# Token blocks of a Strassen-like gate and up product, built in four interleaved steps, and two VectorE operands read from PSUM

## The chip, the cores and the metric

The kernel runs on one core of one Trainium2 chip. The metric is the device time of one execution in microseconds (us); the number given for a kernel is the median of its runs. Engines are named as in the profile: PE is TensorE (matmuls), PEld its weight loads, DVE is VectorE, ACT is ScalarE, POOL is GpSimd, SP the engine whose queue issues the DMAs.

## What is computed

One layer of a streaming encoder on x of 512 tokens by 2048 channels, float32. The part that matters here is its end:

```python
y = jnp.concatenate([y_sb, y_cv, y_sg], axis=-1)          # each normalised per head
x = x + jnp.einsum('bse,ed->bsd', y, w_out[l])            # 2048 x 2048
h = rms_norm(x, ffn_norm[l])
gate = causal_depthwise_conv(jnp.einsum('bsd,df->bsf', h, w_gate[l]), ffn_conv_w[l], ffn_conv_b[l])
up = jnp.einsum('bsd,df->bsf', h, w_up[l])                # d = 2048, f = 5632
x = x + jnp.einsum('bsf,fd->bsd', jax.nn.silu(gate) * up, w_down[l])
return rms_norm(x, final_norm)
```

## The kernel before

Every float32 operand of a matmul is used as two parts, `hi` (the value rounded to TensorE's fp32r format by a cast on ScalarE) and `lo` (value minus `hi`, a subtraction on VectorE), and every product is three matmuls: hi·hi, lo·hi, hi·lo. `split` makes the two parts; `mm3` issues the three matmuls. For sums of weights `make_split` casts twice on ScalarE, once to SBUF (`b_hi`, the operand) and once to a PSUM bank (`b_hp`), and VectorE subtracts the PSUM copy; for raw weights there is one cast and VectorE reads `b_hi` from SBUF.

The W_out stage runs over four blocks `nb` of 512 output columns, each over 16 row blocks of the contraction (`rows_by_weight`, results in four PSUM banks called `po`, of ring `zz` or `mm` in turn). At the end of a block VectorE adds the banks to x, giving `x1[nb][tt]`, ScalarE squares each tile with a sum (`add2`, for the token statistics; the squares go to a tile `junk` that nobody reads), and the tile is stored to DRAM for the last stage.

Gate and up multiply in the Winograd form of Strassen's scheme: seven products of half-size blocks in place of eight. The weight side's sums S1 to S4 are made on GpSimd (`make_sum`). The token side needs, for each of 8 row blocks j, the blocks R11, T1 (`build_a`) and R21, R22, T2, T3, T4 (`build_b`). `build_b(j)` transposes x1 on TensorE (`turned`, tile `ps_tr`), scales it out of PSUM on ScalarE (`f_b`), splits that into `rb`, forms T3 = R22 - R12 on GpSimd and T2 = R22 - T1 on VectorE (tile `t_b`), splits that into `rc`, forms T4 = R21 - T2 and splits it into `rd`. `build_a` of all j and `build_b` of j = 0 to 3 run beside the W_out products (table `WHEN`); `build_b` of j = 4 to 7 needs the last x1 block and is called whole, two blocks ahead of the first product, one after product n = 0 and one after n = 1 (`more_rows`).

The products run over 44 groups g of 256 columns, gate and up in turn, and in a group over 14 half products (i = 0 to 6 of `SEQ`, q = 0 or 1, each 12 matmuls). `order` lists them; its first 28 mix the first two groups so that half products that need late blocks come later. In step n the program issues the weight sum six ahead, the split four ahead, the product, `more_rows(n)` and the steps of the output generators (`gate_out`, `up_out`). The sums X, Y, Z1, Z2 of a group share two PSUM banks; after i = 2 ScalarE copies X to c11 and VectorE adds Y; after i = 3 VectorE makes c22 from Z1 and Z2; after i = 4 ScalarE copies X to u (`ff_u`) and VectorE adds u to c22; c12 and c21 follow from u and Z1, Z2 (all c tiles are called `ff_g` in the trace). i = 4 adds into X again, so it may start only when c11 is out.

ScalarE's instructions stay in program order (`keep_in_program_order`); the order on the other engines and on the DMA queue is set by the framework's scheduler from ready times that it reckons itself. The line that records every engine operation is 105, so groups are told apart by tile names. `token_row` (at n = 6) turns the token statistics (`fin2`, on GpSimd) into `row2`, with eight small matmuls `ps_row`; the gate outputs are multiplied by it.

Of the kernel before, what the change touches and what calls it, by code (L numbers as in the profile page):

```python
# [9 lines left out]
F32 = mybir.dt.float32  # L10
F32R = mybir.dt.float32r
AF = mybir.ActivationFunctionType
ALU = mybir.AluOpType
# [100 lines left out]
def trunk_kernel(  # L114
# [128 lines left out]
    def split(hi, lo, src, hi_eng=None, lo_eng=None):  # L243
        if hi_eng is None:
            act_.copy(hi, src)
        else:
            hi_eng.tensor_copy(hi, src)
        return (lo_eng or vec).tensor_tensor(out=lo, in0=src, in1=hi.bitcast(F32), op=ALU.subtract)
# [106 lines left out]
    def token_stats(name, junk_tile):  # L355

        ssq = const.tile([P, NT, 4], F32, name=f"ssq_{name}")
        rs = const.tile([P, NT], F32, name=f"rstd_{name}")

        def add(tt, b, src):  # L360
            act_.activation(junk_tile(), src, AF.Square, accum_out=ssq[:, tt, b : b + 1])
            return ssq[:, tt, b : b + 1]

        def finish_(tt):
            acc = ssq[:, tt, :]
            pool.tensor_tensor(out=acc[:, 0:2], in0=acc[:, 0:2], in1=acc[:, 2:4], op=ALU.add)
            pool.tensor_tensor(out=acc[:, 0:1], in0=acc[:, 0:1], in1=acc[:, 1:2], op=ALU.add)
            rstd_cols(rs[:, tt : tt + 1], acc[:, 0:1], D)

        return rs, add, finish_  # L370
# [475 lines left out]
        exp_ln_table()  # L846
        iss.spawn(gate_u(half, u), w)

    rstd2, add2, fin2 = token_stats("x1", lambda: tmp("junk"))
    x1 = [[None] * NT for _ in range(4)]  # L850
    x1_dram = [[dram.tile([P, S], F32, name=f"x1_{nb}_{tt}") for tt in range(NT)] for nb in range(4)]

# [13 lines left out]
    tmp_pool = raw_pool = x1_pool = act2 = None  # L866

    def tmp(name):
        return tmp_pool.tile([P, S], F32, tag="tmp", bufs=12, name=name)


    groups = [(w, 256 * fp) for fp in range(NF // 2) for w in (w_gate, w_up)]
# [29 lines left out]
            return act_tile(name)  # L902
        return x1_pool.tile([P, S], F32R, tag="x1", bufs=8, name=name)

    def turned(kt, tag_fn, name):
        ps = tag_fn("ps_tr")
        for tt in range(NT):
            transpose(ps[:, tt * P : (tt + 1) * P], x1[kt // 4][tt][:, (kt % 4) * P : (kt % 4 + 1) * P], ident)
        f = tmp(name)
        act_.activation(f, ps, AF.Copy, scale=gcol(32 + kt))  # L910
        return f

    def halves_of(t):
        return t[:, 0:HT], t[:, HT:S]

    def build_a(j, tag_fn):

        fa[j] = f = turned(j, tag_fn, "f_a")
        hi, lo = r_tile("ra_hi", True), r_tile("ra_lo", True)
        f0, f1 = halves_of(f)  # L920
        for at, name in enumerate(("R11", "T1")):
            if at:
                vec.tensor_tensor(out=f0, in0=f1, in1=f0, op=ALU.subtract)
            h, l = halves_of(hi)[at], halves_of(lo)[at]
            split(h, l, f0)
            R[name, j] = (h, l)

    def build_b(j, tag_fn):

        f, t = turned(j + 8, tag_fn, "f_b"), tmp("t_b")  # L930
        t1, r12 = halves_of(fa.pop(j))
        r21, r22 = halves_of(f)
        t2, t3 = halves_of(t)
        hi, lo = r_tile("rb_hi"), r_tile("rb_lo")
        split(hi, lo, f)
        R["R21", j], R["R22", j] = zip(halves_of(hi), halves_of(lo))
        pool.tensor_tensor(out=t3, in0=r22, in1=r12, op=ALU.subtract)
        vec.tensor_tensor(out=t2, in0=r22, in1=t1, op=ALU.subtract)
        hi, lo = r_tile("rc_hi"), r_tile("rc_lo")
        split(hi, lo, t)  # L940
        R["T2", j], R["T3", j] = zip(halves_of(hi), halves_of(lo))
        vec.tensor_tensor(out=r21, in0=r21, in1=t2, op=ALU.subtract)
        h, l = halves_of(r_tile("rd"))
        split(h, l, r21)
        R["T4", j] = (h, l)

    WHEN = {1: {3: 0, 6: 1, 9: 2, 12: 3}, 2: {3: 4, 6: 5, 9: 6, 12: 7}, 3: {2: 0, 5: 1, 8: 2, 11: 3}}
    for nb in range(4):
        tag_fn, other = (mm, zz) if nb % 2 == 0 else (zz, mm)
        banks = [tag_fn("po") for _ in range(NT)]  # L950
        for n, kt in enumerate(OUT_ORDER):
            if nb == 0 and n + 4 < KT:
                out_operand(OUT_ORDER[n + 4])
            rows_by_weight(banks, yT[kt], n == 0, n == KT - 1)
            if nb == 0 and n == KT - 5:
                open_up_stage()
            if n in WHEN.get(nb, ()):
                (build_b if nb == 3 else build_a)(WHEN[nb][n], other)
            if n == KT - 5:
                for tt in range(NT):  # L960
                    x1[nb][tt] = x1_pool.tile([P, S], F32, tag="x1", bufs=8, name="x1")
                    nc.sync.dma_start(out=x1[nb][tt], in_=x[tt * P : (tt + 1) * P, nb * S : (nb + 1) * S])
        for tt in range(NT):
            vec.tensor_tensor(out=x1[nb][tt], in0=x1[nb][tt], in1=banks[tt], op=ALU.add)
            if nb < 3:
                add2(tt, nb, x1[nb][tt])
            nc.sync.dma_start(out=x1_dram[nb][tt], in_=x1[nb][tt])
        if nb == 2:
            blk_load(0)
    mix_stage.close()  # L970
    sp = up_stage.enter_context(tc.tile_pool(name="split", bufs=1, reuse_waits="tile"))

# [18 lines left out]
    def make_sum(n):  # L991
        g, i, q = UNITS[n]
        name = SEQ[i][0]
        if name in SUMS:
            a, b, op = SUMS[name]
            if g == 1 and (name == "S1" or (name, q) == ("S3", 0)):
                t = tmp("b_sum").rearrange("p (k c) -> p k c", k=4)
            else:
                t = sp.tile([P, 4, P], F32, tag="sum", bufs=5, name="b_sum")
            pool.tensor_tensor(out=t, in0=operand(g, a, q), in1=operand(g, b, q), op=op)  # L1000
            sums[g, name, q] = t

    def make_split(n):
        g, i, q = UNITS[n]
        if i == 0 and q == 0 and g > 0:
            blk_load(g + 1)
        hi = sp.tile([P, 4, P], F32R, tag="bhi", bufs=5, name="b_hi")
        lo = sp.tile([P, 4, P], F32R, tag="blo", bufs=4, name="b_lo")
        src = operand(g, SEQ[i][0], q)
        if SEQ[i][0] in SUMS:  # L1010


            hp = zz("b_hp").rearrange("p (k c) -> p k c", k=4)
            act_.copy(hi, src)
            act_.copy(hp.bitcast(F32R), src)
            vec.tensor_tensor(out=lo, in0=src, in1=hp, op=ALU.subtract)
        else:
            split(hi, lo, src)
        parts[n] = (hi, lo)
# [35 lines left out]
    def product(n):  # L1055
        g, i, q = UNITS[n]
        if g not in banks_of:
            b1, b2 = mm("pt"), mm("pt")
            banks_of[g] = (*halves_of(b1), *halves_of(b2))
        X, Y, Z1, Z2 = banks_of[g]  # L1060
        acc = (X, Z1, Y, Z2, X, Z1, Z2)[i]
        hi, lo = parts.pop(n)
        for kk in range(4):
            rh, rl = R[SEQ[i][1], 4 * q + kk]
            mm3(acc, hi[:, kk, :], lo[:, kk, :], rh, rl, i < 2 and q == 0 and kk == 0, q == 1 and kk == 3)
        if q == 0:
            return
        if i < 2:
            return
        if g not in outs_of:  # L1070
            outs_of[g] = (tmp("ff_g0"), tmp("ff_g1"))
        (c11, c12), (c21, c22) = (halves_of(c) for c in outs_of[g])
        f0 = 2 * (g // 2)
        out_fn = gate_out if g % 2 == 0 else up_out
        if i == 2:
            act_.copy(c11, X)
            vec.tensor_tensor(out=c11, in0=c11, in1=Y, op=ALU.add)
        elif i == 3:
            vec.tensor_copy(c22, Z1)
            vec.tensor_tensor(out=c22, in0=c22, in1=Z2, op=ALU.add)  # L1080
        elif i == 4:
            u_of[g] = tmp("ff_u")[:, 0:HT]
            act_.copy(u_of[g], X)
            vec.tensor_tensor(out=c22, in0=c22, in1=u_of[g], op=ALU.add)
        elif i == 5:
            vec.tensor_tensor(out=c12, in0=u_of[g], in1=Z1, op=ALU.add)
            out_steps.append(out_fn(f0, outs_of[g][0]))
        elif i == 6:
            vec.tensor_tensor(out=c21, in0=u_of[g], in1=Z2, op=ALU.add)
            out_steps.append(out_fn(f0 + 1, outs_of[g][1]))  # L1090
# [17 lines left out]
    blk_load(1)  # L1108
    for n in range(AHEAD):
        make_split(order[n])  # L1110
    build_b(4, zz)
    build_b(5, zz)
    row2 = None

    def more_rows(n):
        nonlocal row2
        if n == 0:
            build_b(6, zz)
        elif n == 1:
            for tt in range(NT):  # L1120
                add2(tt, 3, x1[3][tt])
            build_b(7, zz)
        elif n == 6:
            for tt in range(NT):
                fin2(tt)
            row2 = token_row(rstd2, "x1")
# [163 lines left out]
```

## Time and profile before

| | |
|---|---|
| runs | 2257.87, 2253.45, 2257.39 us; median 2257.39 |
| profiled execution | 2258.5 us; its span on the core 2256.8 us |
| mean granted clock of TensorE | 0.989 of full speed |
| busy | PE 2144.6 us (95%), PEld 1936.0 (86%), DVE 1507.1 (67%), ACT 1213.2 (54%), POOL 777.3 (34%) |
| chain that ended last | PE 83%, DVE 8%, ACT 4%, issue 2%, POOL 1%, DMA 1% |
| DMA | 245.29 MB, mean 109 GB/s; q1 32.8% of 16 engines |
| PE in 40 slices, tenths | 8999999999999879999999999999999799999998 |

A busy share is an average over stages; a slice is 56.4 us. The W_out stage ends near 771 us, gate and up run to about 1730, the down projection to the end. In a list of waits a line reads: engine, tile and line that waited, whom it waited for, us in total, times, the longest. In a timeline the bracket behind an instruction is the idle time of its engine before it and what ended that.

### The profile page before, as it was taken

To read this page: it belongs to the slowest core of one execution; us is meant where nothing else is said; L and a number is where in the kernel's file an instruction comes from. 1 tells how busy PE (TensorE), PEld (TensorE's weight loads), DVE (VectorE), ACT (ScalarE), POOL (GpSimd) and SP (SyncE) were. 2 spreads that over 40 slices of the span, in tenths; PEclk is the share of its full clock that TensorE was granted. 3 is DMA by queue.
4 is the path that set the end of the run, shared out by engine and by line. 5 is a ranking of instruction groups with operands and counts; after the bars stand their busy time and mean duration, and the time that the engine had idled before them with its cause. 6 is when DMAs were issued, how large, how long until landed. Compare 5 with 4: busy or idle time off the path is not lost.

```text
span 2256.8 us, 36249 instructions
## 1 busy us (share of the span) xinstructions
PE 2144.6 (95%) x13529; PEld 1936.0 (86%) x13529; DVE 1507.1 (67%) x2264; ACT 1213.2 (54%) x2260; POOL 777.3 (34%) x699
## 2 busy tenths in 40 slices
PE   8999999999999879999999999999999799999998
PEld 6888888798788779999999999999999688888886
DVE  4789897977734667777777777777777444343335
ACT  5335567676634466666676666666666332232223
POOL 1021232321300356566566566656755000000002
PEclk9999999999999989999999999999999899999999
DMA  5232222222264123333323323333331844332232
GB/s 177 92 94 77 65 75 66 66 61 66 85 220 154 66 72 99 121 105 111 118 94 127 113 94 127 103 109 116 100 122 48 289 150 132 111 122 98 99 108 98
DMA packets 193890, 245.29 MB, mean 109 GB/s; under 512 B 8901, under 2 KB 140849, under 8 KB 193713
## 3 DMA queue, kind: packets, MB, share of 16 engines
q1 hardware_dynamic: 193153, 242.70, 32.8%
q8 instruction: 106, 1.74, 0.3%
q14 instruction: 71, 0.58, 0.1%
q10 hardware_dynamic: 560, 0.27, 0.0%
HBM read 223.01 MB, written 19.92 MB: 108 GB/s over the span
## 4 chain that ended last, share of the span: by engine, by line
PE 83%; DVE 8%; ACT 4%; issue 2%; POOL 1%; DMA 1%; SPq 0%; DVEq 0%; POOLq 0%; ACTq 0%
PE pt L172 48%; PE pd L172 19%; PE po L172 8%; PE pn L172 3%; PE pl L172 2%; DVE cv_acc L105 1%; DVE b_lo L105 1%; DVE w_lo L105 1%; DVE ff_g L105 1%; ACT e L105 1%; PE av L172 1%; PE z_C L172 1%; PE z_A L172 0%; DVE wt_lo L105 0%; PE z_B L172 0%
## 5 line engine op out<-in xcount | busy, mean ns | idle before, releaser
L105 DVE TENSOR_TENSOR w_lo<-w_raw,w_hi 128x512 fp32r<-128x512 f32 x400 | 284.7, 719 | 345.8 <-ACT w_hi L105 342.3
L105 ACT CAST w_hi<-w_raw 128x512 fp32r<-128x512 f32 x400 | 245.3, 621 | 455.5 <-PE pd L172 308.6
L105 DVE TENSOR_TENSOR b_lo<-b_sum,b_hp 128x512 fp32r<-128x512 f32 x352 | 239.6, 685 | 152.1 <-PE pt L172 122.8
L105 DVE TENSOR_TENSOR b_lo<-b_raw,b_hi 128x512 fp32r<-128x512 f32 x264 | 279.6, 1083 | 26.2 <-PE pt L172 17.3
L105 ACT CAST b_hi<-b_sum 128x512 fp32r<-128x512 f32 x352 | 218.1, 620 | 135.6 <-PE pt L172 60.8
L172 PE MATMUL pd<-w_hi,t_hi 128*128 128x512 f32 x640 | 250.3, 391 | 14.2 <-ACT w_hi L105 14.2
L172 PE MATMUL pd<-w_lo,t_hi 128*128 128x512 f32 x640 | 250.1, 391 | 0.0
L172 PE MATMUL pd<-w_hi,t_lo 128*128 128x512 f32 x640 | 249.9, 391 | 0.0
L105 POOL TENSOR_TENSOR b_sum<-b_raw 128x512 f32<-128x512 f32 x176 | 235.0, 1365 | 13.6 <-DVE b_lo L105 5.7
L172 PE MATMUL pt<-rc_hi,b_hi 128*128 128x256 f32 x704 | 201.5, 286 | 25.0 <-DVE ff_g L105 25.0
L172 PE MATMUL pt<-ra_hi,b_lo 128*128 128x256 f32 x704 | 203.1, 289 | 22.9 <-DVE b_lo L105 22.9
L172 PE MATMUL pt<-ra_hi,b_hi 128*128 128x256 f32 x704 | 200.8, 285 | 15.1 <-ACT b_hi L105 15.1
L105 ACT CAST b_hp<-b_sum 128x512 fp32r<-128x512 f32 x352 | 205.7, 584 | 0.7 <-DVE x L105 0.7
L172 PE MATMUL pt<-rb_hi,b_lo 128*128 128x256 f32 x704 | 201.4, 286 | 0.0
L172 PE MATMUL pt<-ra_lo,b_hi 128*128 128x256 f32 x704 | 200.5, 285 | 0.0
L172 PE MATMUL pt<-rc_lo,b_hi 128*128 128x256 f32 x704 | 199.2, 283 | 0.0
L172 PE MATMUL pt<-rb_hi,b_hi 128*128 128x256 f32 x704 | 199.1, 283 | 0.0
L172 PE MATMUL pt<-rc_hi,b_lo 128*128 128x256 f32 x704 | 199.1, 283 | 0.0
L172 PE MATMUL pt<-rb_lo,b_hi 128*128 128x256 f32 x704 | 199.1, 283 | 0.0
L105 POOL TENSOR_TENSOR b_sum<-b_sum,b_raw 128x512 f32<-128x512 f32 x88 | 131.0, 1488 | 193.8 <-DVE b_lo L105 193.7
L105 ACT CAST b_hi<-b_raw 128x512 fp32r<-128x512 f32 x264 | 160.3, 621 | 59.4 <-PE pt L172 33.3
L172 PE MATMUL pt<-hT_hi,w_hi 128*128 128x512 f32 x448 | 175.7, 393 | 0.3 <-ACT hT_hi L105 0.2
(260 smaller groups left out, 5723.2 us busy)
## 6 DMA issues: line engine op xcount, KB each, us to landing
b_raw<-in_w_gate_dram SPq DMA_DIRECT2D x88, 512.0 KB
b_raw<-in_w_up_dram SPq DMA_DIRECT2D x88, 512.0 KB
w_raw<-in_w_down_dram SPq DMA_DIRECT2D x88, 512.0 KB
w_raw<-in_w_in_dram SPq DMA_DIRECT2D x80, 512.0 KB
w_raw<-in_w_out_dram SPq DMA_DIRECT2D x32, 512.0 KB
t<-ff_g SPq DMA_DIRECT2D x44, 256.0 KB
t_raw<-t SPq DMA_DIRECT2D x44, 256.0 KB
x<-in_x_dram SPq DMA_DIRECT2D x32, 256.0 KB
```

Of the source, the lines that this page charges most:

```text
L105: ins = f(*a, **k)
L172: return nc.tensor.matmul(o, lhsT=lhsT, rhs=rhs, start=start, stop=stop, skip_group_check=True)
```

## The change

- `build_b` becomes a generator of four steps: transposes and `f_b`; the cast and subtraction for `rb` with T2 and T3; the split into `rc` with T4; the split into `rd`. T2 and T3 are formed by one VectorE operation over 512 columns (R22 broadcast over the two halves), in place in the `f_a` tile. In W_out block 3 each started block advances by one step per row block. The late blocks j = 4 to 7 advance by the table `ROWS`, two blocks a step from n = 0 to 7.
- The additions and stores of `x1[3]` move behind the first two weight splits of the new stage; its squares move to n = 3 and 4, `fin2` and `token_row` from n = 6 to n = 9.
- `junk` lies in a PSUM bank. The ring of 12 temporary tiles is divided into one of 4 and one of 8 (`tmp_g`: `f_a`, some weight sums of g = 1, the c tiles).
- The splits of L11 (i = 0) of all groups but the first get the second cast into PSUM, and VectorE subtracts from there; c22 adds X straight from PSUM in place of u.

```diff
@@ -846,7 +846,8 @@
         exp_ln_table()
         iss.spawn(gate_u(half, u), w)
 
-    rstd2, add2, fin2 = token_stats("x1", lambda: tmp("junk"))
+    rstd2, add2, fin2 = token_stats("x1", lambda: junk_bank[0]("junk"))
+    junk_bank = [zz]
     x1 = [[None] * NT for _ in range(4)]
     x1_dram = [[dram.tile([P, S], F32, name=f"x1_{nb}_{tt}") for tt in range(NT)] for nb in range(4)]
 
@@ -866,7 +867,10 @@
     tmp_pool = raw_pool = x1_pool = act2 = None
 
     def tmp(name):
-        return tmp_pool.tile([P, S], F32, tag="tmp", bufs=12, name=name)
+        return tmp_pool.tile([P, S], F32, tag="tmp", bufs=4, name=name)
+
+    def tmp_g(name):
+        return tmp_pool.tile([P, S], F32, tag="tmp_g", bufs=8, name=name)
 
 
     groups = [(w, 256 * fp) for fp in range(NF // 2) for w in (w_gate, w_up)]
@@ -902,11 +906,10 @@
             return act_tile(name)
         return x1_pool.tile([P, S], F32R, tag="x1", bufs=8, name=name)
 
-    def turned(kt, tag_fn, name):
+    def turned(kt, tag_fn, f):
         ps = tag_fn("ps_tr")
         for tt in range(NT):
             transpose(ps[:, tt * P : (tt + 1) * P], x1[kt // 4][tt][:, (kt % 4) * P : (kt % 4 + 1) * P], ident)
-        f = tmp(name)
         act_.activation(f, ps, AF.Copy, scale=gcol(32 + kt))
         return f
 
@@ -915,7 +918,7 @@
 
     def build_a(j, tag_fn):
 
-        fa[j] = f = turned(j, tag_fn, "f_a")
+        fa[j] = f = turned(j, tag_fn, tmp_g("f_a"))
         hi, lo = r_tile("ra_hi", True), r_tile("ra_lo", True)
         f0, f1 = halves_of(f)
         for at, name in enumerate(("R11", "T1")):
@@ -927,24 +930,31 @@
 
     def build_b(j, tag_fn):
 
-        f, t = turned(j + 8, tag_fn, "f_b"), tmp("t_b")
-        t1, r12 = halves_of(fa.pop(j))
+        f = turned(j + 8, tag_fn, tmp("f_b"))
+        yield
+        t = fa.pop(j)
         r21, r22 = halves_of(f)
-        t2, t3 = halves_of(t)
+        t2, _ = halves_of(t)
         hi, lo = r_tile("rb_hi"), r_tile("rb_lo")
-        split(hi, lo, f)
+        act_.copy(hi, f)
+        vec.tensor_tensor(
+            out=t.rearrange("p (a c) -> p a c", a=2), in0=r22[:, None, :].to_broadcast([P, 2, HT]),
+            in1=t.rearrange("p (a c) -> p a c", a=2), op=ALU.subtract,
+        )
+        vec.tensor_tensor(out=lo, in0=f, in1=hi.bitcast(F32), op=ALU.subtract)
         R["R21", j], R["R22", j] = zip(halves_of(hi), halves_of(lo))
-        pool.tensor_tensor(out=t3, in0=r22, in1=r12, op=ALU.subtract)
-        vec.tensor_tensor(out=t2, in0=r22, in1=t1, op=ALU.subtract)
+        yield
         hi, lo = r_tile("rc_hi"), r_tile("rc_lo")
         split(hi, lo, t)
         R["T2", j], R["T3", j] = zip(halves_of(hi), halves_of(lo))
         vec.tensor_tensor(out=r21, in0=r21, in1=t2, op=ALU.subtract)
+        yield
         h, l = halves_of(r_tile("rd"))
         split(h, l, r21)
         R["T4", j] = (h, l)
 
     WHEN = {1: {3: 0, 6: 1, 9: 2, 12: 3}, 2: {3: 4, 6: 5, 9: 6, 12: 7}, 3: {2: 0, 5: 1, 8: 2, 11: 3}}
+    building = []
     for nb in range(4):
         tag_fn, other = (mm, zz) if nb % 2 == 0 else (zz, mm)
         banks = [tag_fn("po") for _ in range(NT)]
@@ -955,18 +965,27 @@
             if nb == 0 and n == KT - 5:
                 open_up_stage()
             if n in WHEN.get(nb, ()):
-                (build_b if nb == 3 else build_a)(WHEN[nb][n], other)
+                if nb < 3:
+                    build_a(WHEN[nb][n], other)
+                else:
+                    building.append(build_b(WHEN[nb][n], other))
+            for b in list(building):
+                if next(b, b) is b:
+                    building.remove(b)
             if n == KT - 5:
                 for tt in range(NT):
                     x1[nb][tt] = x1_pool.tile([P, S], F32, tag="x1", bufs=8, name="x1")
                     nc.sync.dma_start(out=x1[nb][tt], in_=x[tt * P : (tt + 1) * P, nb * S : (nb + 1) * S])
+        if nb == 3:
+            break
+        junk_bank[0] = other
         for tt in range(NT):
             vec.tensor_tensor(out=x1[nb][tt], in0=x1[nb][tt], in1=banks[tt], op=ALU.add)
-            if nb < 3:
-                add2(tt, nb, x1[nb][tt])
+            add2(tt, nb, x1[nb][tt])
             nc.sync.dma_start(out=x1_dram[nb][tt], in_=x1[nb][tt])
         if nb == 2:
             blk_load(0)
+    junk_bank[0] = zz
     mix_stage.close()
     sp = up_stage.enter_context(tc.tile_pool(name="split", bufs=1, reuse_waits="tile"))
 
@@ -994,7 +1013,7 @@
         if name in SUMS:
             a, b, op = SUMS[name]
             if g == 1 and (name == "S1" or (name, q) == ("S3", 0)):
-                t = tmp("b_sum").rearrange("p (k c) -> p k c", k=4)
+                t = tmp_g("b_sum").rearrange("p (k c) -> p k c", k=4)
             else:
                 t = sp.tile([P, 4, P], F32, tag="sum", bufs=5, name="b_sum")
             pool.tensor_tensor(out=t, in0=operand(g, a, q), in1=operand(g, b, q), op=op)
@@ -1007,7 +1026,7 @@
         hi = sp.tile([P, 4, P], F32R, tag="bhi", bufs=5, name="b_hi")
         lo = sp.tile([P, 4, P], F32R, tag="blo", bufs=4, name="b_lo")
         src = operand(g, SEQ[i][0], q)
-        if SEQ[i][0] in SUMS:
+        if (i == 0 and g > 0) or SEQ[i][0] in SUMS:
 
 
             hp = zz("b_hp").rearrange("p (k c) -> p k c", k=4)
@@ -1068,7 +1087,7 @@
         if i < 2:
             return
         if g not in outs_of:
-            outs_of[g] = (tmp("ff_g0"), tmp("ff_g1"))
+            outs_of[g] = (tmp_g("ff_g0"), tmp_g("ff_g1"))
         (c11, c12), (c21, c22) = (halves_of(c) for c in outs_of[g])
         f0 = 2 * (g // 2)
         out_fn = gate_out if g % 2 == 0 else up_out
@@ -1081,7 +1100,7 @@
         elif i == 4:
             u_of[g] = tmp("ff_u")[:, 0:HT]
             act_.copy(u_of[g], X)
-            vec.tensor_tensor(out=c22, in0=c22, in1=u_of[g], op=ALU.add)
+            vec.tensor_tensor(out=c22, in0=c22, in1=X, op=ALU.add)
         elif i == 5:
             vec.tensor_tensor(out=c12, in0=u_of[g], in1=Z1, op=ALU.add)
             out_steps.append(out_fn(f0, outs_of[g][0]))
@@ -1108,19 +1127,24 @@
     blk_load(1)
     for n in range(AHEAD):
         make_split(order[n])
-    build_b(4, zz)
-    build_b(5, zz)
+        if n == 1:
+            for tt in range(NT):
+                vec.tensor_tensor(out=x1[3][tt], in0=x1[3][tt], in1=banks[tt], op=ALU.add)
+                nc.sync.dma_start(out=x1_dram[3][tt], in_=x1[3][tt])
+    late_b = {j: build_b(j, zz) for j in range(4, 8)}
+    for j in (4, 5):
+        next(late_b[j])
     row2 = None
+    ROWS = {0: (4, 6), 1: (5, 7), 2: (4, 6), 3: (5, 7), 4: (4, 6), 5: (5, 7), 6: (6,), 7: (7,)}
 
     def more_rows(n):
         nonlocal row2
-        if n == 0:
-            build_b(6, zz)
-        elif n == 1:
-            for tt in range(NT):
+        for j in ROWS.get(n, ()):
+            next(late_b[j], None)
+        if n in (3, 4):
+            for tt in (2 * n - 6, 2 * n - 5):
                 add2(tt, 3, x1[3][tt])
-            build_b(7, zz)
-        elif n == 6:
+        elif n == 9:
             for tt in range(NT):
                 fin2(tt)
             row2 = token_row(rstd2, "x1")
```

## Rows read from the trace of the kernel before

**Rows 1.** Busy time by stretch: span, PE, PEld, DVE, ACT, POOL busy, granted clock, DMA.

```profile
780.00:790.00 10.00, 3.65 (x16) 2.92 (x14) 8.07 (x12) 5.19 (x11) 5.30 (x4) 0.83 0.00 0
790.00:800.00 10.00, 2.24 (x12) 1.74 (x12) 3.01 (x5) 4.33 (x12) 7.38 (x20) 0.59 0.00 1
800.00:812.00 12.00, 10.14 (x66) 9.59 (x67) 6.76 (x11) 8.39 (x16) 2.17 (x4) 0.77 0.01 1
1200.00:1700.00 500.00, 476.58 (x3887) 468.63 (x3886) 385.55 (x536) 326.98 (x604) 315.03 (x231) 1.00 0.34 109
```

**Rows 2.** TensorE's waits, 730 to 860 us: total, times, longest.

```profile
PE pt L172 <- ACT b_hi L105: 15.1, 3, 8.7
PE pt L172 <- DVE b_lo L105: 3.9, 4, 2.1
```

**Rows 3.** TensorE's waits, 860 to 1700 us.

```profile
PE pt L172 <- DVE ff_g L105: 21.6, 20, 1.1
PE pt L172 <- DVE b_lo L105: 18.1, 19, 1.0
```

**Rows 4.** Timeline of TensorE: start, length, instruction, [idle before it, what ended it].

```profile
771.37 0.28 PE L172 MATMUL pt<-ra_hi,b_hi 128*128 128x256 f32 x1
...
774.33 1.47 PE L176 MATMUL ps_tr<-ident,x 128*128 128x128 f32 x12
...
801.23 0.58 PE L172 MATMUL pt<-ra_hi,b_hi 128*128 128x256 f32 x1 [8.67 <-ACT b_hi L105]
...
813.77 0.28 PE L172 MATMUL pt<-rb_hi,b_hi 128*128 128x256 f32 x1
```

**Rows 5.** Timeline of ScalarE at the change of stage.

```profile
774.97 0.69 ACT L105 ACTIVATE f_b<-ps_tr,cols_a 128x512 f32<-128x512 f32 x1 [2.22 <-PE ps_tr L176]
...
798.15 0.62 ACT L105 CAST rc_hi<-t_b 128x512 fp32r<-128x512 f32 x1 [4.41 <-POOL t_b L105]
...
800.57 0.61 ACT L105 CAST b_hi<-b_sum 128x512 fp32r<-128x512 f32 x1
801.09 0.58 ACT L105 CAST b_hp<-b_sum 128x512 fp32r<-128x512 f32 x1
```

**Rows 6.** Timeline of GpSimd at the change of stage.

```profile
790.76 0.47 POOL L105 TENSOR_TENSOR ssq_x<-ssq_x 128x2 f32<-128x2 f32 x2 [2.55 <-ACT junk L105]
...
797.40 0.72 POOL L105 TENSOR_TENSOR t_b<-f_b,f_a 128x256 f32<-128x256 f32 x1
```

**Rows 7.** VectorE's groups, 860 to 1700 us: busy us, mean ns of one.

```profile
L105 DVE TENSOR_TENSOR b_lo<-b_raw,b_hi 128x512 fp32r<-128x512 f32 x232 | 248.7, 1097 | 23.1 <-PE pt L172 15.1 <-issue 8.0
...
L105 DVE TENSOR_TENSOR b_lo<-b_sum,b_hp 128x512 fp32r<-128x512 f32 x312 | 212.3, 685 | 132.1 <-PE pt L172 106.7 <-POOL b_sum L105 11.3 <-issue 10.6
...
L105 DVE TENSOR_TENSOR ff_g<-ff_g,ff_u 128x256 f32<-128x256 f32 x38 | 36.7, 965 | 0.0
...
L105 DVE TENSOR_TENSOR ff_g<-ff_u,pt 128x256 f32<-128x256 f32 x78 | 32.2, 413 | 0.0
```

**Rows 8.** Timeline of VectorE at the end of an up group.

```profile
1267.61 3.22 DVE L105 TENSOR_TENSOR b_lo<-b_raw,b_hi 128x512 fp32r<-128x512 f32 x2
1270.75 1.51 DVE L105 TENSOR_TENSOR ff_g<-ff_g,ff_u 128x256 f32<-128x256 f32 x1
1272.18 1.28 DVE L105 TENSOR_TENSOR b_lo<-b_raw,b_hi 128x512 fp32r<-128x512 f32 x2
```

**Rows 9.** Timeline of the same moment on ScalarE, GpSimd and TensorE.

```profile
1269.16 0.62 ACT L105 CAST b_hi<-b_raw 128x512 fp32r<-128x512 f32 x1
...
1270.24 1.74 POOL L105 TENSOR_TENSOR b_sum<-b_sum,b_raw 128x512 f32<-128x512 f32 x1
...
1272.91 0.39 PE L172 MATMUL pt<-ra_hi,b_lo 128*128 128x256 f32 x1 [0.94 <-DVE b_lo L105]
```

**Rows 10.** ScalarE at the start of an up group.

```profile
1258.04 0.82 ACT L105 ACTIVATE ff_c<-ff_g,cols_f 128x512 f32<-128x512 f32 x1 [3.27 <-DVE ff_g L105]
...
1264.48 0.37 ACT L105 COPY ff_g<-pt 128x256 f32<-128x256 f32 x1
```

## Prediction

> **What bounds the kernel now.** The page's busy line comes first: TensorE is busy for 95% of the span, no other engine for more than 67%, and TensorE's lines make 83% of the chain that ended last. So only time in which TensorE stands still, or runs slowly, is to be had. The slices of the page show two kinds of it. The PE digit is 9 nearly everywhere, with a dip in the 14th and 15th slices (from 733 to 846 us), and the gate and up stage behind it loses a steady few per cent: 476.58 of 500 us busy [rows 1].
>
> The dip is the change of stage from the W_out products to gate and up. Rows 1 cut it into stretches: TensorE works 3.65 of 10 us, then 2.24 of 10, and the granted clock sinks to 0.83, 0.59 and 0.77 behind the idle time, that is, part of the work ran at 1.2 GHz and not at 2.4. The waits of TensorE there [rows 2] name the casts `b_hi`: 15.1 us in 3 waits, the longest 8.7. Why ScalarE is late stands in its own timeline [rows 5]: from 774.97, when the first late `f_b` leaves PSUM, until 800.57, when a `b_hi` comes at last, it works through four calls of `build_b`, each a round trip (ScalarE, GpSimd, ScalarE, VectorE, ScalarE) in a queue kept in program order. The worst place is 798.15: the cast `rc_hi` of the last block has stood 4.41 us behind GpSimd's half of `t_b`, and that stood behind the statistics `fin2` [rows 6], which began at 790.76 and let `t_b` in only at 797.40, 6.6 us later.
>
> In the steady stage TensorE waits for two things [rows 3]: 20 times for `ff_g` (21.6 us, 1.08 each) and 19 times for `b_lo` (18.1 us, 0.95 each). With 44 column groups in pairs of gate and up, that is one wait of each kind in a pair. The `b_lo` wait is the one at 1272.91 [rows 9]. On VectorE [rows 8] the reason stands in front of it: two `b_lo` of raw weights take 3.22 us together, then `ff_g<-ff_g,ff_u` (c22 += u) takes 1.51, and only then, at 1272.18, come the two `b_lo` (L11 of the next group) that TensorE wants. The `ff_g` wait has another cause: ScalarE, in order, stands 3.27 us before an `ff_c` [rows 10] and has caught up only after 1264.48, when it copies X out for c11; VectorE adds Y after that, and TensorE may write X again only then.
>
> **Part 1, the change of stage.** First what TensorE lost. Twelve half products (n = 0 to 11 of `order`) lie between 771.37 and 813.77 [rows 4], 42.4 us. Twelve matmuls each at the steady pace of 476.58 / 3887 = 0.1226 us [rows 1] need 144 x 0.1226 = 17.7 us; 16 transposes and the 8 small matmuls of `token_row` at 1.47 / 12 = 0.12 us [rows 4] add 2.9. So 42.4 - 20.6 = 21.8 us are lost, 15.1 of them in the three waits, the rest in short ones and in the slow clock.
>
> After the change no step of a block waits in the queue for the step just issued: a round trip of one block is covered by splits and by steps of another. GpSimd's `t_b` is gone, so the 4.41 us behind `fin2` cannot come back, and `fin2` moves from n = 6 to n = 9, where nothing on ScalarE waits for GpSimd. The first two `b_lo` are ahead of the x1 additions, so that short wait goes too. ScalarE's total work remains, and it is what then sets the pace. I count what stands in its queue from 774.97 to the last split that n = 11 needs. Splits of units 14 to 17 two casts each, of 4, 6, 18 and 20 one, two, one and two: 14. Four each of `f_b`, `rb_hi`, `rc_hi`, squares: 16. Thirty at the 0.52 from one cast's start to the next [rows 5] are 15.6; the reads of the accumulators behind the squares I estimate at 0.1 each (0.4); four half-width `rd` at 0.3 are 1.2. That is 17.2, so 792.2. One `b_lo` (0.69, [rows 7]) and one half product (12 x 0.1226 = 1.5) later n = 12 starts, at 794.4. I add 1.5 for round trips that stay open and for `token_row`: 796, against 813.8 before. **Gain 18 us.** The bounds: TensorE alone would start n = 12 at 771.4 + 20.6 = 792, a gain of 21.8. From the other side, VectorE.
>
> The single T2/T3 operation goes to VectorE with all 512 columns, both operands in SBUF, in place of 256 there and 256 on GpSimd. VectorE's work in the same stretch: per block three operations of 512 columns and two of 256, 3 x 0.69 + 2 x 0.42 = 2.9, four blocks 11.6, and eight `b_lo` 5.5: 17.1 us, as much as ScalarE. The price of an operation with both operands in SBUF is not firm, though: `b_lo` from `b_raw` and `b_hi` takes 1097 ns on the mean, the same from a sum and a PSUM copy 685 [rows 7]. The Trainium skill, in "SBUF — State Buffer", section "Who interferes with whom", says why: VectorE's second SBUF input comes through a read port shared with GpSimd, so such an operation contends with a GpSimd one that reads SBUF. The rows agree, and the rule speaks against the merged operation, since it is one more of that kind. By row: at the mean of 1097 the 12 operations and two raw splits cost 14 x 0.41 = 5.7 more, and the gain falls to some 13. If every one of them met GpSimd at the 3.22 / 2 = 1.61 of rows 8, it would be 14 x 0.92 = 12.9 more and a gain of 5. That is the lower bound of this part. I stay near the upper end, since four `t_b` leave GpSimd and its sums here are few.
>
> Costed at nothing: `junk` in PSUM. The next column block's banks are then taken by squares just before. What hides them is the last products of the old block, beside which three of the four additions and squares run; without that cover a bank comes late by about one addition and one square, 0.69 + 0.52 = 1.2 us at each of three boundaries [rows 5, 7]. The tile rings (4 and 8 in place of 12) hold a whole pair of groups. The x1 stores pass behind two weight loads in the DMA queue; by my count of ScalarE's queue they are wanted over 10 us later, when the last `rc` and `rd` tiles reuse their memory; if not, the last block waits for them, within the lower bound below.
>
> **Part 2, the steady stage.** c22 += X costs what `ff_g<-ff_u,pt` costs, 413 ns, and not 965 on the mean or the 1.51 of rows 8. At the critical place L11 can then start 1.51 - 0.41 = 1.10 us sooner, at 1271.08, which is more than the 0.94 that TensorE waits [rows 9]. At that time GpSimd still works (1270.24 plus 1.74, to 1271.98, [rows 9]), so from SBUF L11's `b_lo` would be slow; with its copy in PSUM it takes 685 ns [rows 7]. The extra cast is 0.52 us on ScalarE. It follows `b_hi` of 1269.16 and is done by 1270.3, before 1271.08. So nearly all of the 18.1 us goes: **gain 18 us**. Bounds: 0 if VectorE's order puts something else as late in front of L11; 18.1 + 21.6 = 39.7 if the `ff_g` wait falls with it. I see nothing that moves the `ff_g` wait: what delays c11 lies at the start of the up group, where the change adds no work and takes none.
>
> **Sum.** 2258.5 (the profiled execution; its span is 2256.8) - 18 - 18 = 2222.5. The median shown is 1.1 below that execution, so 2221.4, rounded to 2222.
>
> **Rivals.** *One part alone works* (chance 0.20): order on VectorE keeps L11 late, or the late blocks still go one after the other; 2257.4 - 18 = 2239. For it: orders other than ScalarE's aren't fixed by the text. Against it: both waits have a cause that the change removes.
>
> *VectorE becomes the bound at the change of stage, by contention* (0.10): the gain there falls to 5, 2257.4 - 5 - 18 = 2234. This is the case of the port rule above; the trace shows the slow form but also GpSimd's long idle times there.
>
> *The `ff_g` wait goes too* (0.09): 2222 - 21.6 = 2200. Against it: ScalarE's 3.27 us stand [rows 10] has another source.
>
> *Slower: the added casts stay in ScalarE's queue* (0.07). Two per group at 0.52, over 43 groups, are 44.7 us; if no idle time of ScalarE lay between L11's casts and the copy for c11, each would push TensorE's `ff_g` wait by as much, and 2222 + 44.7 = 2267. It decides from 36 / 44.7, that is, when four fifths of them come through. Against it: the 3.27 us of idle lie just between [rows 10], and TensorE waits in no place of the steady stage for ScalarE itself [rows 3].
>
> *No visible effect* (0.04): the time lost in both places returns at the next wait; 2257.
>
> **How the numbers follow.** The forecast has 0.50. About 0.2% (4.5 us) is what a measurement of this kernel can tell from no change. Its own spread is 2213 to 2230. The range 2204 to 2241 takes in the forecast, the one-part case and the contention case, and leaves out the case of 2200, the slower one and no effect, 0.20 together. Faster by over 0.2%: 0.50 + 0.20 + 0.10 + 0.09 = 0.89; within: 0.04; slower: 0.07.
>
> **What would show it.** In the trace after: the three `b_hi` waits of TensorE between 772 and 802 gone or under 2 us each, the granted clock near 1.00 there, n = 12 at about 796; one `ff_g` operation with X from PSUM at about 0.41 us; the `b_lo` waits of the steady stage gone and the 20 of `ff_g` left. The prediction is wrong if a wait of over 4 us stays behind a late block, if `token_row` holds TensorE for GpSimd's 6.6 us, or if a new wait of 0.9 us in each pair takes the place of the old.

## The result, and the profile after

The changed kernel takes 2218.93 us at the median (2216.73 to 2221.07, 4 runs), before 2256.97 (4 runs): ratio 0.9834, 95% interval [0.9817, 0.9851]. The forecast was 2222, in a range from 2204 to 2241. The profiled execution is one of 2221.07 us with a span of 2219.3, against 2256.8 before.

Busy time by stretch of the changed kernel at the change of stage and in the steady stage (columns as in [rows 1]):

```profile
780.00:790.00 10.00, 7.58 (x59) 6.97 (x59) 9.93 (x15) 9.98 (x24) 6.86 (x8) 1.00 0.00 0
790.00:800.00 10.00, 7.21 (x52) 6.74 (x52) 6.50 (x13) 7.00 (x15) 9.15 (x17) 0.93 0.01 2
...
1200.00:1660.00 460.00, 449.19 (x3681) 443.57 (x3681) 355.01 (x502) 326.80 (x610) 298.31 (x218) 1.00 0.36 114
```

The stretch from 780 to 800, in which TensorE worked 5.9 of 20 us before [rows 1], now has 14.8, at a granted clock of 1.00 and 0.93. VectorE and ScalarE are busy for 9.93 and 9.98 of 10 us from 780 to 790: they are full there, and TensorE still has holes. TensorE's waits, 730 to 830 us, then 860 to 1700:

```profile
PE pt L172 <- DVE b_lo L105: 4.1, 5, 1.4
PE pt L172 <- DVE ff_g L105: 2.2, 1, 2.2
PE ps_row L172 <- POOL diag L105: 2.2, 1, 2.2
```

```profile
PE pt L172 <- DVE ff_g L105: 21.4, 20, 1.1
```

The three `b_hi` waits of 15.1 us [rows 2] are gone, and so are all 19 `b_lo` waits of the steady stage [rows 3]; the 20 of `ff_g` stand. TensorE's timeline: the first products, `token_row` with the start of n = 12, and the start of n = 28:

```profile
772.12 0.28 PE L172 MATMUL pt<-ra_hi,b_hi 128*128 128x256 f32 x1
...
773.67 0.39 PE L172 MATMUL pt<-ra_hi,b_lo 128*128 128x256 f32 x1 [1.15 <-DVE b_lo L105]
...
784.25 0.39 PE L172 MATMUL pt<-ra_hi,b_lo 128*128 128x256 f32 x1 [1.40 <-DVE b_lo L105]
...
795.85 0.60 PE L172 MATMUL ps_row<-diag,ones_f 128*128 128x128 f32 x4
...
798.78 1.22 PE L172 MATMUL ps_row<-diag,ones_f 128*128 128x128 f32 x4 [2.21 <-POOL diag L105]
...
801.08 0.41 PE L172 MATMUL pt<-rb_hi,b_hi 128*128 128x256 f32 x1
...
828.70 0.40 PE L172 MATMUL pt<-rd,b_hi 128*128 128x256 f32 x2
```

From its first product to n = 12 TensorE took 28.96 us (772.12 to 801.08), before 42.40 [rows 4]: 13.4 gained. From n = 12 to n = 28 it took 27.6, before 29.5 (813.77 to 843.28): 1.9 more. The first product itself starts 0.75 later than before. So the change of stage is worth 13.4 + 1.9 - 0.75 = 14.6 us. For the steady stage, here are two `ff_g` waits, 15 pairs of groups apart:

```profile
1030.50 0.39 PE L172 MATMUL pt<-rc_hi,b_hi 128*128 128x256 f32 x1 [1.08 <-DVE ff_g L105]
...
1662.40 0.39 PE L172 MATMUL pt<-rc_hi,b_hi 128*128 128x256 f32 x1 [1.06 <-DVE ff_g L105]
```

A pair takes (1662.40 - 1030.50) / 15 = 42.13 us; before, the same two waits stood at 1006.31 and 1654.90, 43.24 a pair. That is 1.11 a pair and 22.2 over 20 pairs. The whole stretch from n = 28 to the start of the last product matmul of gate and up agrees: 907.6 us before (843.28 to 1750.83) and 885.3 now (828.70 to 1713.98), 22.3 less. So that stage ends near 1751 before the change, not near the 1730 given above. 14.6 + 22.2 = 36.8 of the 37.5 us between the two spans.

### The profile page after: what moved, and what is told of

The parts are those of the page before. It is cut to its first block, busy times and chain, and to the rows that moved or that the text cites. A ratio compares the mean times of both kernels' runs of the same rounds, so it can differ in the third digit from the quotient of the medians.

```text
span 2219.3 us, 36258 instructions
## 1 busy us (share of the span) xinstructions
PE 2139.5 (96%) x13529; PEld 1933.9 (87%) x13529; DVE 1489.7 (67%) x2264; ACT 1248.1 (56%) x2346; POOL 774.2 (35%) x691
## 4 chain that ended last, share of the span: by engine, by line
PE 83%; DVE 7%; ACT 5%; issue 2%; DMA 1%; POOL 1%; SPq 0%; ACTq 0%; POOLq 0%; DVEq 0%
PE pt L172 48%; PE pd L172 20%; PE po L172 7%; PE pn L172 3%; PE pl L172 2%; DVE cv_acc L105 1%; DVE w_lo L105 1%; ACT b_hi L105 1%; PE av L172 1%; ACT e L105 1%; ACT b_hp L105 1%; PE z_C L172 1%; DVE ff_g L105 1%; DVE b_lo L105 1%; PE z_A L172 1%
## 5 line engine op out<-in xcount | busy, mean ns | idle before, releaser
L105 DVE TENSOR_TENSOR b_lo<-b_raw,b_hi 128x512 fp32r<-128x512 f32 x178 | 224.9, 1290 | 2.0 <-PE pt L172 1.5
```

What stands on the lines that cost most here:

```text
L105: ins = f(*a, **k)
```

## The experiments

All are run against the kernel before; each ratio is of that, so a difference of two ratios is known to about 0.2%, or 5 us. In all 12 TensorE has the same number of matmuls.

**Do the two parts add up?** The first run undoes the PSUM operands in the changed kernel, the second makes them alone in the kernel before.

```diff
-        if (i == 0 and g > 0) or SEQ[i][0] in SUMS:
+        if SEQ[i][0] in SUMS:
...
-            vec.tensor_tensor(out=c22, in0=c22, in1=X, op=ALU.add)
+            vec.tensor_tensor(out=c22, in0=c22, in1=u_of[g], op=ALU.add)
```

> The changed kernel with both PSUM operands undone: L11 is split as raw weights again and c22 adds u. If the two parts of the change add up (my theory), this keeps the change of stage's part alone, some 15 us by the two traces: about 2242 us, with TensorE's 19 or so waits for b_lo of 0.95 us back in the steady stage. The rival, that the steady gain comes from the division of the tile rings or from another order of instructions, expects about 2220 and no such waits.

Measured: 2240.64, ratio 0.9934 [0.9919, 0.9949].

> The kernel before with the two PSUM operands alone. If the parts add up: about 22 us under before, 2235, with the b_lo waits of the steady stage gone, and the three b_hi waits of 15 us at the change of stage still there. The rival, that the PSUM operands need the rest of the change, expects 2257 and the b_lo waits unchanged.

Measured: 2234.63, ratio 0.9906 [0.9891, 0.9921]. TensorE's `b_lo` waits in the first run (860 to 1660 us), and its `b_hi` waits in the second (765 to 860 us):

```profile
PE pt L172 <- DVE b_lo L105: 18.3, 19, 1.0
```

```profile
PE pt L172 <- ACT b_hi L105: 13.9, 3, 7.9
```

Each part leaves the other's waits where they were, and in the second run no `b_lo` wait is left between 860 and 1660 us. Their gains, 0.66% and 0.94%, make 1.60% together, and the whole change has 1.66% [1.49, 1.83]. The rivals, that the tile rings or the order do it, fall.

**Which of the two PSUM operands?** One of the two lines of the diff above at a time, in the changed kernel.

> The changed kernel with L11 split as raw weights (VectorE reads both operands from SBUF), c22 still from PSUM. My theory: VectorE reaches L11 1.1 us earlier, but beside GpSimd's sum, so the subtraction takes 1.3 to 1.6 us in place of 0.69 and most of the b_lo wait returns, 0.5 to 0.9 in each pair: 2229 to 2237 us. The rival, that c22 alone is what counts, expects 2219 and no b_lo waits.

Measured: 2235.37, ratio 0.9911 [0.9894, 0.9927].

> The changed kernel with c22 adding u from SBUF again, L11's copy in PSUM kept. My theory: c22 takes about 1.5 us again at the critical place, L11 starts 1.1 us later and the b_lo wait of 0.9 returns: about 2238 us. The rival, that L11's copy is what counts, expects 2219 and no b_lo waits.

Measured: 2240.85, ratio 0.9933 [0.9918, 0.9947]. The `b_lo` waits of the steady stage, first without L11's copy, then with c22 from u:

```profile
PE pt L172 <- DVE b_lo L105: 12.0, 19, 0.6
```

```profile
PE pt L172 <- DVE b_lo L105: 18.2, 19, 1.0
```

0.63 a wait without L11's copy, 0.96 with c22 from u, none with both. L11's copy by itself is worth nothing (2240.85 against 2240.64 with neither operand in PSUM). c22 by itself takes away a third of the wait and some 5 of the 22 us (2235.37). It takes both, as the VectorE timeline of the changed kernel shows (the place of [rows 8]):

```profile
1243.04 3.25 DVE L105 TENSOR_TENSOR b_lo<-b_raw,b_hi 128x512 fp32r<-128x512 f32 x2
1246.21 0.41 DVE L105 TENSOR_TENSOR ff_g<-ff_g,pt 128x256 f32<-128x256 f32 x1
1246.54 1.40 DVE L105 TENSOR_TENSOR b_lo<-b_raw,b_hp 128x512 fp32r<-128x512 f32 x2
```

c22 += X takes 0.41 us in place of 1.51, and the two `b_lo` of L11 come right behind it, at 1.40 us for two, beside GpSimd.

**token_row.** It holds TensorE for 2.21 us at 798.78, and the matmuls behind it run at the lower clock (granted 0.50 from 799.60 to 801.60, that is 1.2 GHz). The edit puts `elif n == 13` for `elif n == 9`.

> The changed kernel with fin2 and token_row at n = 13 in place of 9. In its trace TensorE stands 2.2 us in the middle of token_row for GpSimd's diag and then runs some 2 us at the lower clock. If that is a cost of its own (my theory), TensorE reaches the 145th product matmul about 3 us sooner after the first and the time is 2 to 4 us less. The rival, that the wait only moves (row2 is then late for the first gate output), expects no difference or a wait for ff_g in its place.

Measured: 2219.44, ratio 0.9837 [0.9821, 0.9854]: no difference. TensorE's timeline:

```profile
802.39 0.84 PE L172 MATMUL ps_row<-diag,ones_f 128*128 128x128 f32 x4 [2.12 <-POOL diag L105]
...
817.55 0.38 PE L172 MATMUL pt<-rc_hi,b_hi 128*128 128x256 f32 x1 [3.01 <-DVE ff_g L105]
```

The wait is as long as before (2.12), only later: `fin2` moved together with `token_row`, so GpSimd's last `diag` is later too. The clock stays at 1.00 behind it this time. n = 12 does come 25.31 us after the first product (771.12 to 796.43) and not 28.96, but n = 28 comes 56.69 after it against 56.58, and the `ff_g` wait of the first pair grows from 2.2 to 3.0 us. The gain that I expected is not there, and the rival, that the time returns at the next wait, has it right. But the edit moved the wait and did not remove it, so it does not show what the wait costs by itself. Other runs leave that open: with c22 from u, and with the steps alone, TensorE stands only 0.3 us in `token_row`, and n = 28 comes 53.96 and 56.53 us after the first product.

**Interleaving or the merged operation?** The first of these runs builds the late blocks whole.

```diff
-        next(late_b[j])
+        list(late_b[j])
...
-        for j in ROWS.get(n, ()):
-            next(late_b[j], None)
-        if n in (3, 4):
-            for tt in (2 * n - 6, 2 * n - 5):
+        if n == 0:
+            list(late_b[6])
+        elif n == 1:
+            for tt in range(NT):
                 add2(tt, 3, x1[3][tt])
+            list(late_b[7])
```

> The changed kernel with the late blocks built whole again, two ahead of the first product, one after n = 0, and after n = 1 the squares and the last one, as before the change; T2 and T3 stay one VectorE operation, and fin2 stays at n = 9. If the interleaving is what pays (theory A), the b_hi waits come back but for the 4.4 us behind GpSimd: 8 to 12 us slower than the changed kernel, about 2229. If the merged operation off GpSimd is what pays (theory B), the time stays within 3 us of 2219.

Measured: 2229.54, ratio 0.9884 [0.9869, 0.9899]. The second forms T3 on GpSimd, in steps; the third does so with whole blocks.

```diff
-        vec.tensor_tensor(
-            out=t.rearrange("p (a c) -> p a c", a=2), in0=r22[:, None, :].to_broadcast([P, 2, HT]),
-            in1=t.rearrange("p (a c) -> p a c", a=2), op=ALU.subtract,
-        )
+        pool.tensor_tensor(out=t[:, HT:S], in0=r22, in1=t[:, HT:S], op=ALU.subtract)
+        vec.tensor_tensor(out=t2, in0=r22, in1=t2, op=ALU.subtract)
```

> The changed kernel with T3 formed by GpSimd and T2 by VectorE in the same steps. Theory A (interleaving pays): GpSimd's 1 us is hidden behind other steps, the time stays within 3 us of 2219. Theory B (the merged operation pays): rc_hi stands behind GpSimd's sums, and 5 to 12 us come back.

Measured: 2219.85, ratio 0.9839 [0.9824, 0.9854].

> The run with the late blocks built whole, and T3 formed by GpSimd again. With steps interleaved, T3 on GpSimd cost nothing. If the 4.4 us that the whole blocks with the merged operation kept of the gain came from rc_hi no longer standing behind fin2 on GpSimd, they are lost here: 4 to 6 us slower than whole blocks with the merged operation, about 2234. The rival, that they came from other edits, expects 2229.

Measured: 2236.62, ratio 0.9913 [0.9898, 0.9928]. TensorE's `b_hi` waits with whole blocks (765 to 860 us), and ScalarE's last `rc_hi` with whole blocks and T3 on GpSimd:

```profile
PE pt L172 <- ACT b_hi L105: 10.0, 3, 5.9
```

```profile
800.76 0.62 ACT L105 CAST rc_hi<-f_a 128x512 fp32r<-128x512 f32 x1 [3.21 <-POOL f_a L105]
```

Whole blocks bring 10.0 us of `b_hi` waits back, so theory A holds: interleaving is worth about 0.5%, 11 us, with the merged operation, and 0.74%, 17 us, with T3 on GpSimd. The merged operation is worth 0.29% (0.9913 against 0.9884, some 6.5 us, known to 5) where blocks are whole, and nothing where they are interleaved. That `rc_hi` otherwise stands behind GpSimd (3.21 us in that row) is the likely reason: the `b_hi` waits are 14.0 us there, 4.0 more. The traces, one of each, say the same of this stretch:

| from the first product to n = 28, us | T3 on GpSimd | merged operation |
|---|---|---|
| blocks whole | 71.67 | 67.50 |
| blocks interleaved | 55.72 | 56.58 (the changed kernel) |

The kernel before takes 71.91. So whole blocks with T3 on GpSimd give back all that was gained in this stretch: none of the other edits there (`fin2` later, the tile rings, the place of the additions) shows a gain by itself.

**The ff_g wait.** In up groups VectorE copies X to c11:

```diff
-            act_.copy(c11, X)
+            if g % 2:
+                vec.tensor_copy(c11, X)
+            else:
+                act_.copy(c11, X)
```

> The changed kernel with the copy of X to c11 made by VectorE in up groups, by ScalarE in gate groups as it was. My theory of the ff_g wait, that ScalarE's lateness delays c11: VectorE is free when X is ready, so the 20 waits of 1.07 us go and the time falls by 18 to 23 us, to about 2198. The rival, that VectorE is as late as ScalarE there or the wait moves to another operand, expects 2214 to 2222 and waits of the same sum.

Measured: 2218.81, ratio 0.9837 [0.9822, 0.9852]. The waits of the steady stage, and VectorE's timeline in front of L11:

```profile
PE pt L172 <- DVE b_lo L105: 23.2, 19, 1.2
```

```profile
1241.49 3.53 DVE L105 TENSOR_TENSOR b_lo<-b_raw,b_hi 128x512 fp32r<-128x512 f32 x2
1244.95 0.41 DVE L105 TENSOR_TENSOR ff_g<-ff_g,pt 128x256 f32<-128x256 f32 x1
1245.28 1.27 DVE L105 TENSOR_TENSOR b_lo<-b_raw,b_hp 128x512 fp32r<-128x512 f32 x2
```

The cause was right as far as it goes: with the copy off ScalarE no `ff_g` wait is left. The gain was not: 1.2 us a pair are lost again at L11, behind two L22 subtractions that take 3.53 us. So the next run gives L22 the PSUM copy as well:

```diff
-        if (i == 0 and g > 0) or SEQ[i][0] in SUMS:
+        if (i in (0, 6) and g > 0) or SEQ[i][0] in SUMS:
```

> The changed kernel with X copied to c11 by VectorE in up groups, and L22 (i = 6) too split from a PSUM copy. In the run with c11 on VectorE alone the 20 ff_g waits were gone and 19 b_lo waits of 1.2 us stood in their place: VectorE's two L22 subtractions from SBUF took 3.5 us beside GpSimd's sums, in front of L11. My theory: with L22 from PSUM they take 1.3, both waits are gone, 1.1 us less in each pair: 20 to 24 us under the changed kernel, about 2197. The rival, that ScalarE's two casts more in each group make it late, expects 2215 or more and waits for b_hi or b_lo.

Measured: 2204.91, ratio 0.9773 [0.9759, 0.9788]: a version better than both kernels, 0.6% below the changed one. Its waits, VectorE in front of L11, GpSimd at that moment, TensorE at two waits 15 pairs apart, and the busy line of the steady stage:

```profile
PE pt L172 <- DVE b_lo L105: 3.2, 20, 0.2
```

```profile
1236.65 0.69 DVE L105 TENSOR_TENSOR b_lo<-b_raw,b_hp 128x512 fp32r<-128x512 f32 x1 [0.28 <-ACT b_hp L105]
1237.69 0.69 DVE L105 TENSOR_TENSOR b_lo<-b_raw,b_hp 128x512 fp32r<-128x512 f32 x1 [0.35 <-ACT b_hp L105]
...
1239.01 0.69 DVE L105 TENSOR_TENSOR b_lo<-b_raw,b_hp 128x512 fp32r<-128x512 f32 x1 [0.29 <-ACT b_hp L105]
```

```profile
1235.00 3.87 POOL L105 TENSOR_TENSOR b_sum<-b_raw 128x512 f32<-128x512 f32 x3
```

```profile
1032.77 0.39 PE L172 MATMUL pt<-ra_hi,b_lo 128*128 128x256 f32 x1 [0.16 <-DVE b_lo L105]
...
1653.70 0.39 PE L172 MATMUL pt<-ra_hi,b_lo 128*128 128x256 f32 x1 [0.17 <-DVE b_lo L105]
```

```profile
1200.00:1640.00 440.00, 437.94 (x3578) 431.26 (x3578) 321.88 (x498) 332.30 (x622) 281.28 (x212) 1.00 0.36 117
```

The wait for L11 is down to 0.16 us and a pair takes (1653.70 - 1032.77) / 15 = 41.40 us, 0.73 less. I expected 1.1; part of it is lost again at this wait, in front of which VectorE now stands for ScalarE's casts (0.28 to 0.35 us). TensorE is busy for 437.94 of 440 us, so there is almost nothing left to take from waits in this stage.

Another way at the same wait is a second `yield` in `gate_out` ahead of the bias step, alone and with L22's copy:

> The changed kernel with one more step in gate_out between its multiplication by row2 and ScalarE's bias step, so that ScalarE, in order, has one split's casts ahead of it to work on and doesn't stand 3.9 us for VectorE. My theory of the ff_g wait (ScalarE's lateness comes from that place) expects the 20 waits gone, but, as in the run with c11 on VectorE, a b_lo wait of about 1.1 us in their place: 2215 to 2222. The rival, that the lateness has another source, expects the ff_g waits unchanged.

Measured: 2222.37, ratio 0.9850 [0.9833, 0.9866].

> The same later bias step, and L22 too split from a PSUM copy. My theory: neither wait is left, 20 to 24 us under the changed kernel, about 2197. The rival, that ScalarE's casts make it late again, expects the ff_g waits back and 2215 or more.

Measured: 2223.03, ratio 0.9854 [0.9839, 0.9868]. The waits of the steady stage (860 to 1660 us) without L22's copy and with it, then VectorE's and ScalarE's work at the second bias step without it:

```profile
PE pt L172 <- DVE ff_g L105: 13.3, 20, 0.7
PE pt L172 <- DVE b_lo L105: 9.1, 19, 0.5
```

```profile
PE pt L172 <- DVE ff_g L105: 13.0, 19, 0.7
PE pt L172 <- DVE b_lo L105: 8.8, 18, 0.5
```

```profile
1231.86 1.76 DVE L105 TENSOR_TENSOR b_lo<-b_raw,b_hi 128x512 fp32r<-128x512 f32 x1
1233.54 0.68 DVE L105 TENSOR_TENSOR ff_g<-ff_g,row_x 128x512 f32<-128x512 f32 x1
```

```profile
1234.25 0.82 ACT L105 ACTIVATE ff_c<-ff_g,cols_f 128x512 f32<-128x512 f32 x1 [4.45 <-DVE ff_g L105]
```

Both of my expectations failed. The `ff_g` wait shrinks from 1.07 to 0.67 and does not go, and a `b_lo` wait of 0.48 comes with it; that one stands in front of a product with `rc` (1237.29) and not at L11, so L22's copy leaves it. ScalarE still stands 4.45 us for VectorE's multiplication by row2, which comes behind an L12 subtraction of 1.76 us. The same two operations in the changed kernel:

```profile
1020.24 0.86 DVE L105 TENSOR_TENSOR b_lo<-b_raw,b_hi 128x512 fp32r<-128x512 f32 x1
1021.02 1.78 DVE L105 TENSOR_TENSOR ff_g<-ff_g,row_x 128x512 f32<-128x512 f32 x1
```

There the multiplication is the slow one, and the two take 2.56 us together (1020.24 to 1022.80) against 2.36. Both read two SBUF operands and run beside GpSimd. That they make ScalarE's idle time is argued from these rows; no run sped them up.

## Why the prediction was right

**The place and the cause of both gains** were as forecast, and the two parts are independent, as the first two runs show. That the sum is so near is luck: two sizes were off in opposite directions, by 3.4 and 4.2 us. Two small slips of the working change nothing: 18 - 5.7 is 12.3 and not "some 13", and 2221.4 rounds to 2221.

**Part 1 was mis-sized by 3.4 us: 18 forecast, 14.6 measured.** The count of ScalarE's queue held almost to the tenth. I counted 17.2 us from the first late `f_b` to the cast that n = 11 needs; ScalarE's timeline shows 775.73 to 792.47 + 0.58 = 793.05, or 17.3 (with three `rd` before it, not four):

```profile
775.73 1.27 ACT L105 ACTIVATE f_b<-ps_tr,cols_a 128x512 f32<-128x512 f32 x2 [2.22 <-PE ps_tr L176]
...
782.18 0.63 ACT L105 CAST rc_hi<-f_a 128x512 fp32r<-128x512 f32 x1
...
792.47 0.58 ACT L105 CAST b_hp<-b_sum 128x512 fp32r<-128x512 f32 x1
```

`rc_hi` no longer waits for anything. What failed is what I put behind it, "1.5 for round trips that stay open and for token_row". n = 12 started at 801.08 and not 796. Most of that is `token_row`, named as what could make the prediction wrong: from 795.85 on, TensorE had its 8 small matmuls and 7 of n = 11 to do, 15 x 0.12 = 1.8 us, and took 5.23, with a stand of 2.21 us for GpSimd and the matmuls behind it at the lower clock. Besides, "the first two b_lo are ahead of the x1 additions" did not come true (the wait of 1.15 us at 773.67 is in place; the scheduler still puts the additions first), and the first product is 0.75 later. The run with `token_row` later moves this loss behind n = 12 and does not remove it. The 1.9 us gained from n = 12 to n = 28 were not in the forecast. With VectorE and ScalarE both full from 780 to 790, what remains is their work. Which operation would have to go was not tried.

"GpSimd's t_b is gone, so the 4.41 us behind fin2 cannot come back" is true and explains less than I gave it: in steps, T3 on GpSimd costs nothing (2219.85).

**Part 2 was mis-sized by 4 us: 18 forecast, 22.2 measured.** I priced 19 `b_lo` waits at their idle time, 0.95 each. The window from 860 to 1700 left one out: from n = 28 to the end of the stage there are 20, of 19.0 us. And the pair became 1.11 shorter, more than a wait's idle time. TensorE at the start of L11, before and after:

```profile
1012.29 0.28 PE L172 MATMUL pt<-ra_lo,b_hi 128*128 128x256 f32 x1
1013.53 0.39 PE L172 MATMUL pt<-ra_hi,b_lo 128*128 128x256 f32 x1 [0.96 <-DVE b_lo L105]
```

```profile
1036.47 0.28 PE L172 MATMUL pt<-ra_lo,b_hi 128*128 128x256 f32 x1
1036.60 0.39 PE L172 MATMUL pt<-ra_hi,b_lo 128*128 128x256 f32 x1
1036.82 0.28 PE L172 MATMUL pt<-ra_hi,b_hi 128*128 128x256 f32 x1
```

From start to start the two matmuls stood 1.24 us apart with a listed wait of 0.96, and stand 0.13 apart now. The list counts idle time from the end of the matmul in front, which is 0.28 long, while without a wait the next one starts 0.12 after that one's start. So each wait also cost 0.16 of overlap: 19.0 + 20 x 0.16 = 22.2, all that was measured. L11's 1.10 us sooner and the protection by its copy are borne out by the runs with one operand each: c22 alone leaves 0.63 us of the wait, L11's copy alone all of it.

**The port rule.** Two L22 subtractions with both operands in SBUF take 3.53 us beside GpSimd, and 0.69 each with one in PSUM (the runs with c11 on VectorE). The rule of the Trainium skill ("SBUF — State Buffer", "Who interferes with whom") that the prediction names agrees with that. As a rival for the change of stage (a gain of only 5) it did not come in that size: 14.6 were measured. A part of it came. These are GpSimd and VectorE in the changed kernel in front of TensorE's longest `b_lo` wait there, 1.40 us at 784.25:

```profile
778.55 4.77 POOL L105 TENSOR_TENSOR b_sum<-b_raw 128x512 f32<-128x512 f32 x3 [0.94 <-DMA b_raw<-in_w_up_dram]
```

```profile
780.38 1.79 DVE L105 TENSOR_TENSOR f_a<-f_b,f_a 128x512 f32<-128x512 f32 x1
782.10 1.50 DVE L105 TENSOR_TENSOR f_b<-f_b,f_a 128x256 f32<-128x256 f32 x1
783.52 0.67 DVE L105 TENSOR_TENSOR b_lo<-b_raw,b_hp 128x512 fp32r<-128x512 f32 x1
```

Once those sums are done, the same two operations take 0.68 and 0.41 (784.72 and 785.32). So beside the sums they took 2.2 us more, by an estimate from these rows, and that covers the whole wait.

**The `ff_g` wait** stayed, as forecast, and its cause was named rightly as far as c11 goes: with the copy on VectorE it vanishes. Why ScalarE is late is argued from the run with the later bias step; no run removed just VectorE's slow operations. The slower rival (casts piling up in ScalarE's queue) didn't occur even with twice as many added casts.

**Costed at nothing:** `junk` in PSUM and the tile rings. The first product came 0.75 us late, but no cost follows from that: with the program up to there as in the changed kernel, it starts anywhere from 769.73 to 772.31 in nine traces (before: 771.37, in one). A cost of that size is neither shown nor excluded.

## What to carry to other kernels

When one engine runs a chain of round trips in a fixed order, interleaving the chains can pay more than making one step faster: here interleaving took 11 us or more, and the faster step nothing once the chains were interleaved. A wait that is removed in front of a nearly full engine is often paid at the next one: look which operation comes next there, and remove both, as c22 with L11's copy and c11 with L22's copy. Price a stall of TensorE by the change from start to start, not by its listed idle time alone.

## What the runs showed of the hardware

A VectorE subtraction of 128 x 512 takes 0.69 us with one operand in PSUM in the rows above, beside GpSimd's sums too, and up to 3.53 us for two, 1.77 each, with both in SBUF beside those sums. The extra ScalarE cast of 0.58 us that avoids it cost no time where it was added alone (2240.85 us with L11's copy, 2240.64 without). In a stream of 256-column matmuls that start 0.12 us apart, a listed wait of 0.96 us cost 1.11.
